# A feed-forward block in 7 products per pair: the second token pair's columns in reverse, a raw weight pair kept, and layer two's rows in step order

## Chip, cores and metric

One core of one Trainium2 chip. The metric is the device time of one launch in microseconds (us), lower is better; it is the median of several runs.

## What is computed

One decoder layer for one sequence of 2048 tokens and 1024 features, all float32:

```python
h = x + concat[rmsnorm(pool_mix(u)), rmsnorm(stick_breaking_attention(q, k, v))] @ w_out
h = h + relu(rmsnorm(h) @ w_up) ** 2 @ w_down      # d_ff = 4096: the FFN
y = rmsnorm(h)
```

The change lies in the second line, the FFN. "Layer one" is the product with `w_up`, "layer two" the product with `w_down`.

## The kernel before, in words

**Precision.** Every float32 operand of a product is split into a high and a low part (`split`, L143 to L147: ScalarE writes the high part, L146; VectorE the rest, L147), and each product takes three matmuls: high by high, high by low, low by high.

**Pairs of token tiles.** The tokens lie in four tiles of 512 (`T`). The FFN takes them as two pairs, `PAIRS = ((0, 1), (3, 2))`, and multiplies the 2 by 2 blocks of a pair by a 2 by 2 blocked weight with seven products (`P1` to `P7`) in place of eight, so sums and differences of operands (`S1` to `S4`, `A11`, `A12`, `A22`) are made, stored and loaded again. `q` is the pair, 0 or 1.

**Layer one, `up` (L861).** It runs over 32 columns, `cols`: for each pair `q`, the columns m = 0, 8, 1, 9, ..., 7, 15. A column has seven slots, one for each product, each of 12 matmuls of 128x128 by 128x512. For a column, `load` brings the raw weights `rb` (1 MB; one place for m below 8, one for the rest), two columns ahead; `make_weights` sums and splits them four slots ahead (`hw`). The left operands of a pair, `sa`, stay on chip for its 16 columns; `make_left` loads each as two tiles `sr` of 512 KB from `su` and splits them, five slots ahead of the first use, so at the turn from pair 0 to pair 1 fourteen loads and splits fall into the last column of the one and the first of the other. The pool `srp` of the `sr` tiles has three places of 4 KB.

`post` takes a product out of PSUM after its slot: copies `p1`, `u2`, `u3` on ScalarE (`copy`, L1007), the squared relu on ScalarE (L1001, L1002), sums on VectorE, each result in a 2 KB place of the pool `avp` (13 places), and a store to `sd`. For three of the operands (`A22`, `S1`, `A12`) the products of layer two are split a second time by the same scheme, with rows of pair 0 as the one half: in pair 1, `inner_row` loads their rows of pair 0 (`hr`, out of `sd[0]`), into the halves of one `srp` tile for the columns m and m + 8, and `inner_sums` makes from them and the new result what is stored to `sdi`.

While pair 0 runs, `weights_first` prepares part of layer two's weights (loads `t` and `b` of `w_down`, stores to `td` and `wi`) with tiles of `avp`.

**Layer two, `down` (L1090).** `steps` lists P1, P6, P7 with eight steps each over the inner blocks `kk`, in the order `TURN`, then three inner products of 28 steps, then P3. A step of P1, P6 or P7 has 48 matmuls. `make` loads its weights (`wr`) and its rows of both pairs (`ar`, out of `sd`, 512 KB each) and splits them. `make_ahead` makes up to three steps ahead of the one that is multiplied; `more_weights` (through the list `late`) prepares weights of later products. Step 0 is made early, at high priority; the rest of `make_ahead` is queued behind the last store of `S3` (`marks["up"]`, set in `post`).

**Places.** Layer two's pools lie over those of layer one: the first two places of `ar` (`rs`) over the raw weights, the other three (`rs2`) over `srp`, the second pool of split rows (`s82`) over the left operand of P3.

**What sets the order.** A scheduler that simulates the program orders the instructions of each engine; `tc.issue_after(ins)` only keeps what is in its block behind `ins` in the order of the same engine. Almost all DMAs of these stages are issued by SyncE (SP), in one order, and each engine works through its own list in order.

Of the kernel before, what the change touches and what calls it, by code (L numbers as in the profile page):

```python
# [8 lines left out]
F32 = mybir.dt.float32  # L9
# [6 lines left out]
P = 128  # L16
S = 2048
D = 1024
T = 512
# [18 lines left out]
LB = 4  # L38
# [8 lines left out]
def hymba_block(ctx: ExitStack, tc: tile.TileContext, xT, gains, w_in, pool_w, w_out, w_up, w_down, out):  # L47
    nc = tc.nc
# [87 lines left out]
    sd = [[[dram.tile([P, 2, T], F32, name=f"sd{q}_{i}_{c}") for c in range(8)] for i in range(7)] for q in range(2)]  # L136
# [6 lines left out]
    def split(dst, src):  # L143

        hi, lo = dst
        nc.scalar.activation(hi, src, AF.Copy)  # L146
        return nc.vector.tensor_tensor(lo, src, hi.bitcast(F32), ALU.subtract)  # L147
# [5 lines left out]
    marks, gates = {}, []  # L153
# [687 lines left out]
    A11, A12, A22, S1, S2, S3, S4 = range(7)  # L841
# [19 lines left out]
    def up(pools, more):  # L861

        saps, hlp, rba, rtp, srp = pools
        NM = NF // 2
        cols = [(q, m + x * (NM // 2)) for q in range(2) for m in range(NM // 2) for x in range(2)]
        halves = {}

        def inner_row(m, i):

            if m < NM // 2:  # L870
                halves[i, "rows"] = srp.tile([P, 2, T], F32, tag="sr", name="hr")
            nc.sync.dma_start(halves[i, "rows"][:, m // (NM // 2)], sd[0][i][m // 2][:, m % 2])

        def inner_sums(m, i, t):

            rows, at = halves[i, "rows"], m % (NM // 2)
            d, r = rows[:, 0], rows[:, 1]
            keep = lambda n, v: nc.sync.dma_start(sdi[i][n][at // 2][:, at % 2], v)
            if m < NM // 2:
                nc.vector.tensor_tensor(d, d, t, ALU.subtract)  # L880
                keep(2, d)
                halves[i] = t
                return
            a = halves.pop(i)
            nc.vector.tensor_tensor(a, a, t, ALU.add)
            keep(0, a)
            nc.vector.tensor_tensor(d, t, d, ALU.subtract)
            keep(1, d)
            nc.vector.tensor_tensor(r, r, d, ALU.subtract)
            keep(3, r)  # L890
# [5 lines left out]
        order = list(what)  # L896

        slots = [cols[0] + ("P1",)]
# [4 lines left out]
        raw, sums, ops, left_ops, ps, keep = {}, {}, {}, {}, {}, {}  # L903

        def load(q, m):
            raw[q, m] = (rbb if m >= NM // 2 else rba).tile([P, 4, G, P], F32, tag="rb", name="rb")
            nc.sync.dma_start(raw[q, m], w_up[m])

# [79 lines left out]
        def post(q, m, s):  # L988
            k = keep.setdefault((q, m), {})
            x, y, z = (ps.get((q, m, b)) for b in "XYZ")  # L990
            new = lambda name: avp.tile([P, T], F32, tag="av", name=name)

            def put(i, t, kept=None):
                if q == 0 or m >= NM // 2 or i not in (A12, A22, S1):
                    kept = nc.sync.dma_start(sd[q][i][m // 2][:, m % 2], t)
                if q and i in (A12, A22, S1):
                    inner_sums(m, i, t)
                return kept

            def act_of(i, src, t):  # L1000
                nc.scalar.activation(t, src, AF.Relu)  # L1001
                nc.scalar.activation(t, t, AF.Square)  # L1002
                k[i] = t

            def copy(name):
                k[name] = pup.tile([P, T], F32, tag=name, name=name)
                nc.scalar.activation(k[name], y, AF.Copy)  # L1007

            if s == "P1":
                copy("p1")  # L1010
            elif s == "P2":
                t = new("a11")
                nc.vector.tensor_tensor(t, x, k["p1"], ALU.add)
                act_of(A11, t, t)
                put(A11, t)
            elif s == "P6":
                if q:
                    for i in (A22, S1, A12):
                        inner_row(m, i)
                copy("u2")  # L1020
            elif s == "P7":
                copy("u3")
                t = new("a22")
                nc.vector.tensor_tensor(t, z, k["u3"], ALU.add)  # L1024
                act_of(A22, t, t)
                put(A22, t)
            elif s == "P4":
                t = new("a21")
                act_of("A21", y, t)
                k[S1] = new("s1")  # L1030
                nc.vector.tensor_tensor(k[S1], t, k[A22], ALU.add)
                put(S1, k[S1])
                k[S2] = new("s2")
                nc.vector.tensor_tensor(k[S2], k[S1], k[A11], ALU.subtract)
                put(S2, k[S2])
                nc.vector.tensor_tensor(t, k[A11], t, ALU.subtract)
                marks["up"] = put(S3, t)
            elif s == "P3":
                t = new("a12")
                nc.vector.tensor_tensor(t, z, k["u2"], ALU.add)  # L1040
                act_of(A12, t, t)
                put(A12, t)
                s4 = new("s4")
                nc.vector.tensor_tensor(s4, t, k[S2], ALU.subtract)
                put(S4, s4)
# [9 lines left out]
        yield  # L1055
        rbb, pup, avp, psu = more()
        load(*cols[1])
        first_weights = weights_first()
        lefts = [(g, q, s) for g, (q, m, s) in enumerate(slots) if m == 0 and not (q == 0 and s in order[:LB])]
        for g, (q, m, s) in enumerate(slots):  # L1060
            while lefts and lefts[0][0] <= g + LA:
                make_left(*lefts.pop(0)[1:])
# [4 lines left out]
            bank, first, last = what[s][2:]  # L1067
            if first:
                ps[q, m, bank] = psu.tile([P, T], F32, tag=bank, name="p" + bank)
            t, w = ps[q, m, bank], ops.pop(g)  # L1070
# [8 lines left out]
            elif g in (6, 10):  # L1079
                pr, i = psu.tile([P, T], F32, tag="R", name="pr"), g // 10  # L1080
                spread(pr, yrlast[:, i])
                nc.scalar.activation(rlast[:, i], pr, AF.Copy)
            if g + UA < len(slots):
                make_weights(g + UA)
                q2, m2, s2 = slots[g + UA]
                n = cols.index((q2, m2)) + 2
# [3 lines left out]
    def down(pools):  # L1090
        t8, s8, rs, rt, pupa, pup, rtx, rlp, tmp_, psb = pools

        SPLIT = {"P4": A22, "P5": S1, "P2": A12}
        TURN = (0, 4, 1, 5, 2, 6, 3, 7)
        order = (("P1", A11), ("P6", S2), ("P7", S3), ("P4", A22), ("P5", S1), ("P2", A12))
        steps = []
        for n, i in order:
            if n in SPLIT:
                steps += [(n, p, kk, None) for p in ("P1", "P5", "P6", "P3", "P7", "P2", "P4") for kk in range(4)]
            else:  # L1100
                steps += [(n, i, kk, (0, 1)) for kk in TURN]
        steps += [("P3", S4, kk, (q,)) for q in range(2) for kk in range(8)]
        made, turns = {}, {"ar": -2, "ad": 0}

# [27 lines left out]
        def blk(i, kk, where=None):  # L1132
            t = (where or rt).tile([P, 4, 256], F32, tag="wr", name="wr")
            nc.sync.dma_start(t, w_down[i, kk] if isinstance(i, int) else td[int(i[1]) - 1][kk])
            return t

        def minus(a, b):
            nc.vector.tensor_tensor(b, a, b, ALU.subtract)
            return b
# [30 lines left out]
        def make(g):  # L1170
            n, i, kk, qs_ = steps[g]
            if qs_ is None:
                made[g] = make_inner(n, i, kk)
                return
            b11, b12, b21, b22 = range(4)
            if n == "P1":
                w = blk(b11, kk)
            elif n == "P6":
                w = minus(blk(b22, kk), blk("t1", kk))
            elif n == "P7":  # L1180
                w = minus(blk(b22, kk), blk(b12, kk))
            else:
                w = blk(b22, kk)
            rows = {q: row([P, 2, T], F32, "ar") for q in qs_}
            for q in qs_:
                last[0] = nc.sync.dma_start(rows[q], sd[q][i][kk])
            t = t8.tile([P, 2, 4, 256], F32R, tag="wd", name="wd", align_bytes=256)
            split((t[:, 0], t[:, 1]), w)
            left_ = {}
            for q in qs_:  # L1190
                left_[q] = row([P, 2, 2, T], F32R, "ad", align_bytes=256)
                last[1] = split((left_[q][:, 0], left_[q][:, 1]), rows[q])
            while late and n != "P1":
                late.pop(0)()
            late.append(lambda: more_weights(n, kk, w))
            made[g] = t, left_
# [175 lines left out]
        free, held, ahead, late, last = 4, [], [0, 0, 0], [], [None, None]  # L1372
# [10 lines left out]
        def make_ahead(limit=len(steps)):  # L1383

            while ahead[0] < limit and (ahead[1] + lefts(ahead[0]) <= 6 and ahead[2] + stationary(ahead[0]) <= 3):
                make(ahead[0])
                ahead[1] += lefts(ahead[0])
                ahead[2] += stationary(ahead[0])
                ahead[0] += 1

        with tc.high_priority():
            make_ahead(1)
        with tc.issue_after(marks["up"].ins):
            make_ahead()
        for g, (n_, i, kk, qs_) in enumerate(steps):
            t, left_ = made.pop(g)
# [204 lines left out]
```

## Time and profile before

| what | value |
|---|---|
| median of 3 runs | 1921.9 us (1920.15 to 1922.53) |
| the profiled execution's own time | 1928.76 us |
| its span, first to last instruction | 1926.9 us |
| mean granted TensorE clock | 0.993 |
| PE (matmuls) busy | 1896.0 us, 98% |
| VectorE (DVE) / ScalarE (ACT) busy | 1423.0 us, 74% / 1006.2 us, 52% |
| moved by DMA | 511.78 MB, mean 266 GB/s |
| layer one in the trace | about 697 to 1318 us |
| turn from pair 0 to pair 1 | about 1003 us |
| layer two, to the end | from about 1318 us |

In the rows of the profile an engine's line gives start, duration, engine, line of the kernel, and out<-in by the names above; PE is the matmul, PEld its weight load, SPq the issuing of DMAs by SyncE. A bracket gives the idle time before an instruction and what ended it. Windows give the busy time of each engine in a stretch, the granted clock (PEclk, 1.00 is full) and the DMA engines' busy share and rate.

### The profile page before, as it was taken

How to read it: one execution, taken by the hardware profiler on the slowest of the kernel's cores; microseconds unless marked ns; L12 is line 12 of the kernel's file. 1: busy time of each engine (PE TensorE's matmuls, PEld its weight loads, DVE VectorE, ACT ScalarE, POOL GpSimd, SP SyncE). 2: the span in 40 equal slices, each digit the busy share in tenths (PEclk: the TensorE clock that was granted, in tenths of full speed). 3: DMA queues.
4: the chain of work that ended last, by engine and by line, in shares of the span. 5: the costliest groups of instructions: out<-in, count | busy, mean ns of one | idle time of the engine just before them, and what ended most of it. 6: DMA issues, size and time to landing. Idle time of an engine off the chain costs nothing.

```text
span 1926.9 us, 26520 instructions
## 1 busy us (share of the span) xinstructions
PE 1896.0 (98%) x8995; PEld 1581.0 (82%) x8995; DVE 1423.0 (74%) x2128; ACT 1006.2 (52%) x1598; POOL 177.3 (9%) x399
## 2 busy tenths in 40 slices
PE   9999999999999999999999999998999999999997
PEld 7888888887888888888878888886888888888886
DVE  6887799668866977777777877786655447888874
ACT  5565566555554465555566555454233345656543
POOL 0211123101211020000000000000010010020120
PEclk9999999999999999999999999999999999999999
DMA  6686686888797867776786777778998889899862
GB/s 213 206 268 195 201 284 219 259 303 266 268 337 283 299 219 265 279 242 224 275 306 237 265 251 259 247 264 307 357 362 293 279 260 311 287 298 342 295 208 90
DMA packets 206322, 511.78 MB, mean 266 GB/s; under 512 B 24288, under 2 KB 30432, under 8 KB 202080
## 3 DMA queue, kind: packets, MB, share of 16 engines
q1 hardware_dynamic: 201424, 501.33, 75.3%
q0 software_dynamic: 4608, 8.39, 2.4%
q8 instruction: 73, 1.20, 0.3%
q14 instruction: 73, 0.60, 0.1%
q10 hardware_dynamic: 144, 0.26, 0.0%
HBM read 337.92 MB, written 171.97 MB: 265 GB/s over the span
## 4 chain that ended last, share of the span: by engine, by line
PE 85%; DMA 7%; DVE 5%; issue 1%; ACT 1%; SPq 1%; POOL 0%; DVEq 0%; ACTq 0%
PE pb L1409 16%; PE pY L1074 15%; PE pb L1238 10%; PE pd L178 8%; PE pd L180 8%; PE pd L179 8%; PE pZ L1074 7%; PE pX L1074 4%; PE po L675 2%; DMA ar<-sd 1%; PE pta L664 1%; DMA t<-in_w_down_dram 1%; DMA ar<-sdi 1%; PE pm L205 1%; PE pr L231 1%
## 5 line engine op out<-in xcount | busy, mean ns | idle before, releaser
L1074 PE MATMUL pY<-sa,hw 128*128 128x512 f32 x1536 | 368.4, 391 | 4.0 <-ACT u L1007 4.0
L1409 PE MATMUL pb<-ad,wd 128*128 128x512 f32 x1488 | 342.6, 391 | 5.4 <-ACT ad L146 5.3
L1074 PEld LDWEIGHTS pY<-sa,hw 128*128 128x128 f32 x1536 | 289.9, 189 | 65.2 <-ACT u L1007 4.8
L1409 PEld LDWEIGHTS pb<-ad,wd 128*128 128x128 f32 x1488 | 279.5, 188 | 64.8 <-ACT ad L146 6.2
L178 PE MATMUL pd<-h,hl 128*128 128x512 f32 x752 | 299.6, 398 | 0.7 <-DVE qkr L424 0.7
L180 PE MATMUL pd<-h,hl 128*128 128x512 f32 x752 | 297.0, 395 | 0.0
L179 PE MATMUL pd<-h,hl 128*128 128x512 f32 x752 | 296.7, 395 | 0.0
L1238 PE MATMUL pb<-ad,wd 128*128 128x512 f32 x1008 | 228.9, 389 | 0.3 <-DVE ad L147 0.3
L1238 PEld LDWEIGHTS pb<-ad,wd 128*128 128x128 f32 x1008 | 189.1, 188 | 40.0 <-DVE ad L147 0.7
L147 DVE TENSOR_TENSOR ad<-ar,ad 128x1024 fp32r<-128x1024 f32 x148 | 179.5, 1221 | 51.8 <-ACT ad L146 51.8
L146 ACT ACTIVATE ad<-ar 128x1024 fp32r<-128x1024 f32 x148 | 155.1, 1052 | 102.3 <-issue 47.7
L1074 PE MATMUL pZ<-sa,hw 128*128 128x512 f32 x768 | 186.9, 390 | 0.6 <-DVE a L1024 0.6
L1074 PEld LDWEIGHTS pZ<-sa,hw 128*128 128x128 f32 x768 | 144.3, 188 | 31.0 <-DVE a L1024 1.1
L178 PEld LDWEIGHTS pd<-h,hl 128*128 128x128 f32 x752 | 142.2, 189 | 28.2 <-DVE qkr L424 1.0
L180 PEld LDWEIGHTS pd<-h,hl 128*128 128x128 f32 x752 | 141.9, 189 | 27.9
L179 PEld LDWEIGHTS pd<-h,hl 128*128 128x128 f32 x752 | 141.9, 189 | 27.1
L146 ACT ACTIVATE hl<-raw 128x512 fp32r<-128x512 f32 x168 | 104.2, 630 | 110.9 <-PE pd L180 68.8
L147 DVE TENSOR_TENSOR hl<-raw,hl 128x512 fp32r<-128x512 f32 x168 | 114.2, 686 | 55.0 <-ACT hl L146 51.8
L147 DVE TENSOR_TENSOR hw<-rt,hw 128x512 fp32r<-128x512 f32 x128 | 86.8, 685 | 56.4 <-ACT hw L146 56.4
L146 ACT ACTIVATE wd<-wr 128x1024 fp32r<-128x1024 f32 x40 | 42.4, 1060 | 125.9 <-PE pb L1409 99.3
L1001 ACT ACTIVATE a<-a 128x512 f32<-128x512 f32 x96 | 59.4, 630 | 88.4 <-DVE a L1040 40.1
L147 DVE TENSOR_TENSOR wd<-wr,wd 128x1024 fp32r<-128x1024 f32 x40 | 49.0, 1224 | 70.9 <-ACT wd L146 70.8
(219 smaller groups left out, 2696.6 us busy)
## 6 DMA issues: line engine op xcount, KB each, us to landing
ar<-sd SPq DMA_DIRECT2D x100, 512.0 KB, 5.5
rb<-in_w_up_dram SPq DMA_DIRECT2D x32, 1024.0 KB, 6.3
wr<-in_w_down_dram SPq DMA_DIRECT2D x64, 512.0 KB, 5.4
sd<-a SPq DMA_DIRECT2D x112, 256.0 KB, 4.2
raw<-in_w_in_dram SPq DMA_DIRECT2D x50, 512.0 KB, 4.3
ar<-sdi SPq DMA_DIRECT2D x48, 512.0 KB, 5.8
sd<-s SPq DMA_DIRECT2D x88, 256.0 KB, 4.4
sdi<-hr SPq DMA_DIRECT2D x72, 256.0 KB, 4.4
```

Source lines behind the costliest of these rows:

```text
L146: nc.scalar.activation(hi, src, AF.Copy)
L147: return nc.vector.tensor_tensor(lo, src, hi.bitcast(F32), ALU.subtract)
L178: nc.tensor.matmul(ps, hl[:, 0, c], hi, start=(k == 0), stop=False)
L179: nc.tensor.matmul(ps, hl[:, 0, c], lo, start=False, stop=False)
L180: mm = nc.tensor.matmul(ps, hl[:, 1, c], hi, start=False, stop=(k == n - 1))
L205: marks["pm"] = nc.tensor.matmul(pm[:, c:c + 1], ss[:, c * P:(c + 1) * P], inv[n], start=(i == 0), stop=(i == len(parts) - 1))
L231: mm = nc.tensor.matmul(pr[:, b * P:(b + 1) * P], yr[:, x, b:b + 1].to_broadcast([P, P]), identr, start=(b == 0 and x == 0), stop=(b == TB ...
L675: nc.tensor.matmul(po[:, p * 256 + to:p * 256 + to + hi - lo], vw[:, 2 * p + v], at[:, x, lo:hi], start=(p == 0 and n == 0 and x == 0), sk ...
L1001: nc.scalar.activation(t, src, AF.Relu)
L1074: nc.tensor.matmul(t, w[:, wx, c], a[:, ax, c % 2], start=first and c == 0 and x == 0, stop=last and c == G - 1 and x == 2, skip_group_che ...
L1238: nc.tensor.matmul(b, t[:, wx, 2 * (kk % 2) + c, i * P:(i + 1) * P], a[:, ax, c], start=p in ("P1", "P5", "P2") and kk == 0 and c == 0 and ...
L1409: nc.tensor.matmul(ps[q, n], block(t, wx, c, n), left_[q][:, ax, c], start=(n_ in ("P1", "P3") and kk == 0 and c == 0 and x == 0), stop=(n ...
```

## The change

Five things are done together.

- Pair 1 takes the columns in reverse: 7, 15, 6, 14, ..., 0, 8. Its first two columns are the last two of pair 0, so their raw weights are still on chip and `load` takes the tile that is there (no transfer).
- In these two first columns of pair 1 the rows `hr` go to 2 KB places of `avp` instead of halves of an `srp` tile. In the other columns nothing changes there.
- Layer two's P1, P6, P7 take their steps in the order 3, 7, 2, 6, 1, 5, 0, 4, which is the order in which pair 1 now finishes its rows. "First step" and "last step" are counted by place in the list, so `TURN` is looked up in `make`.
- Step 1 of layer two is made behind the last store of `A22` (`marks["A22"]`) and the rest behind that of `S3` (`marks["S3"]`); before, all but step 0 came behind that of `S3`.
- In P1 each row load is queued behind the row load of the operand before it.

```diff
-        cols = [(q, m + x * (NM // 2)) for q in range(2) for m in range(NM // 2) for x in range(2)]
+        cols = [(q, m + x * (NM // 2)) for q in range(2) for m in range(NM // 2)[::(1, -1)[q]] for x in range(2)]
...
-            if m < NM // 2:
-                halves[i, "rows"] = srp.tile([P, 2, T], F32, tag="sr", name="hr")
-            nc.sync.dma_start(halves[i, "rows"][:, m // (NM // 2)], sd[0][i][m // 2][:, m % 2])
+            if m == NM // 2 - 1:
+                halves[i, "rows"] = [avp.tile([P, T], F32, tag="av", name="hr")]
+            elif m == NM - 1:
+                halves[i, "rows"].append(avp.tile([P, T], F32, tag="av", name="hr"))
+            elif m < NM // 2:
+                t = srp.tile([P, 2, T], F32, tag="sr", name="hr")
+                halves[i, "rows"] = [t[:, 0], t[:, 1]]
+            nc.sync.dma_start(halves[i, "rows"][m // (NM // 2)], sd[0][i][m // 2][:, m % 2])
...
-            d, r = rows[:, 0], rows[:, 1]
+            d, r = rows[0], rows[-1]
...
         def load(q, m):
+            if q and m % (NM // 2) == NM // 2 - 1:
+                raw[q, m] = raw[0, m]
+                return
...
-                put(A22, t)
+                marks["A22"] = put(A22, t)
...
-                marks["up"] = put(S3, t)
+                marks["S3"] = put(S3, t)
...
-        lefts = [(g, q, s) for g, (q, m, s) in enumerate(slots) if m == 0 and not (q == 0 and s in order[:LB])]
+        lefts = [(g, q, s) for g, (q, m, s) in enumerate(slots) if (q, m) in ((0, 0), (1, NM // 2 - 1)) and not (q == 0 and s in order[:LB])]
...
-        TURN = (0, 4, 1, 5, 2, 6, 3, 7)
+        TURN = (3, 7, 2, 6, 1, 5, 0, 4)
...
-                steps += [(n, i, kk, (0, 1)) for kk in TURN]
+                steps += [(n, i, kk, (0, 1)) for kk in range(8)]
...
+            if n != "P3":
+                kk = TURN[kk]
...
-                last[0] = nc.sync.dma_start(rows[q], sd[q][i][kk])
+                with tc.issue_after(last[0].ins) if n == "P1" and last[0] else nullcontext():
+                    last[0] = nc.sync.dma_start(rows[q], sd[q][i][kk])
...
-        with tc.issue_after(marks["up"].ins):
+        with tc.issue_after(marks["A22"].ins):
+            make_ahead(2)
+        with tc.issue_after(marks["S3"].ins):
             make_ahead()
```

## The prediction, made before the change was run

> **What bounds the kernel now.** I read the page's first part, then who waited on PE, then PE's timeline in the two places that the change touches (the turn from pair 0 to pair 1, the passage from layer one to layer two), then what stood in front of the late operand there.
>
> ```profile
> PE 1896.0 (98%) x8995; PEld 1581.0 (82%) x8995; DVE 1423.0 (74%) x2128; ACT 1006.2 (52%) x1598; POOL 177.3 (9%) x399
> ```
> ```profile
> PE pb L1409 <- ACT ad L146: 5.3, 2, 4.0
> PE pY L1074 <- ACT u L1007: 4.0, 2, 3.3
> ```
>
> PE is the bound. The change adds and removes no matmul, so it can only win what PE loses by waiting and by the slow clock behind a wait, and can lose only where it makes new waits. The two largest waits lie where the change works: at the turn (L1074, 3.3 us at once) and at the passage (L1409, 5.3 us in two).
>
> ```profile
> 1002.94 2.88 PE L1074 MATMUL pX<-sa,hw 128*128 128x512 f32 x12
> 1009.14 5.49 PE L1074 MATMUL pY<-sa,hw 128*128 128x512 f32 x12 [3.32 <-ACT u L1007]
> ...
> 1022.99 5.60 PE L1074 MATMUL pY<-sa,hw 128*128 128x512 f32 x24
> ```
> ```profile
> 1315.01 2.88 PE L1074 MATMUL pZ<-sa,hw 128*128 128x512 f32 x12
> 1317.73 11.04 PE L1409 MATMUL pb<-ad,wd 128*128 128x512 f32 x48
> 1330.09 11.53 PE L1409 MATMUL pb<-ad,wd 128*128 128x512 f32 x48 [1.32 <-ACT ad L146]
> 1345.64 54.55 PE L1409 MATMUL pb<-ad,wd 128*128 128x512 f32 x232 [4.02 <-ACT ad L146]
> ```
> ```profile
> core 0: us, PE busy (x) PEld busy (x) DVE busy (x) ACT busy (x) POOL busy (x), PEclk, DMA share, GB/s
> 462.30:465.60 3.30, 3.30 (x10) 2.65 (x9) 2.67 (x4) 1.18 (x2) 0.00 (x0) 0.50 0.97 345
> 978.00:988.00 10.00, 10.00 (x46) 8.28 (x45) 6.78 (x12) 7.77 (x13) 0.00 (x0) 1.00 0.91 315
> 1001.00:1008.00 7.00, 4.82 (x22) 3.66 (x20) 4.60 (x7) 0.66 (x2) 0.00 (x0) 1.00 0.98 361
> 1315.60:1322.00 6.40, 6.40 (x30) 5.31 (x29) 5.35 (x9) 1.97 (x4) 0.00 (x0) 1.00 0.90 288
> 1328.00:1345.00 17.00, 12.24 (x52) 9.16 (x50) 7.35 (x6) 6.41 (x7) 0.00 (x0) 1.00 1.03 402
> 1345.60:1349.70 4.10, 4.06 (x11) 2.97 (x12) 4.08 (x4) 3.79 (x4) 0.00 (x0) 0.58 0.45 153
> ```
>
> Twelve matmuls take 2.72 us when nothing is late (1315.01 to 1317.73), so 24 take 5.44 and a layer-two step of 48 takes 10.88. From that, what PE loses:
>
> - The turn. The 12 of 1002.94 would hand over at 1005.66; the next come at 1009.14: 3.48 us. From 1009.14 to 1022.99 the timeline has 48 matmuls: 13.85 us in place of 10.88, 2.97 us lost to the half clock behind the wait. Together **6.45 us**.
> - The passage. Step 1 of layer two starts at 1330.09 in place of 1317.73 + 10.88 = 1328.61: 1.48 us. Step 2 starts 15.55 us behind step 1: 4.67 us more. Behind it the clock is 0.58 for 4.10 us: 0.42 x 4.10 = 1.72 us. Together **7.87 us**.
>
> So 14.32 us, 0.74% of the span, is all that can be won here.
>
> **The change part by part. The turn.** What came last there:
>
> ```profile
> 987.86 0.69 DVE L980 TENSOR_TENSOR t<-t,b 128x512 f32<-128x512 f32 x1 [2.07 <-DMA t<-in_w_down_dram]
> ```
> ```profile
> 991.46 4.42 DMA sr<-su
> ...
> 1000.35 7.17 DMA sr<-su
> ...
> 1007.54 1.06 ACT sa L146
> 1008.60 0.49 ACT u L1007
> ```
> ```profile
> 978.04 0.33 SPq L907 DMA_DIRECT2D rb<-in_w_up_dram  x1
> 996.21 0.33 SPq L907 DMA_DIRECT2D rb<-in_w_up_dram  x1
> ```
>
> PE waits for a PSUM bank that ACT has to copy out (`u`), and ACT, which works in order, stands in front of that copy at the split of a left operand whose load takes 7.17 us, against 4.42 for the one at 991.46. The two `rb` loads are the raw weights of pair 1's first two columns, exactly those that the change drops. The first stands ahead of the load of `t` for which DVE idles 2.07 us; at 315 GB/s its 1.05 MB is 3.3 us of DMA time, of which the chain can gain 2.07 (the idle time) and no more is counted. The second is ahead of the load at 1000.35; 1.05 MB at 361 GB/s is 2.9 us, and 7.17 less the 4.42 of the undisturbed one is 2.75; I take 2.75. The operand then lands at 1007.52 - 2.07 - 2.75 = 1002.7 in place of 1007.52, and with 1.06 and 0.49 of ACT the bank is free at 1004.3, ahead of 1005.66. If only the second counts, it is 1006.3 and 0.7 us stay. Gain 5.7 to 6.45 us; I take **6.2**. What is late next is the left operand of P7, of which the second half is loaded behind the same queue; it moves by the same amounts.
>
> **The `hr` rows.** Six of the 13 `avp` places are taken for parts of the first two columns. The row loads get a wait that they lacked: they read what pair 0 stored one and two columns before, not sixteen. On SP the left-operand loads, stores and the next `rb` stand behind them, and DVE's L880 waits for them; cover is a column of 19 us (7 slots of 2.72) against a landing of 4.2 us for the store and about as much for the load. So nothing for that, and for the fuller pool this row and this one:
>
> ```profile
> 804.24 2.11 PE L1074 MATMUL pZ<-sa,hw 128*128 128x512 f32 x8 [0.63 <-DVE a L1024]
> ```
> ```profile
> ar<-sd SPq DMA_DIRECT2D x100, 512.0 KB, 5.5
> ...
> sd<-a SPq DMA_DIRECT2D x112, 256.0 KB, 4.2
> ```
>
> At 804 `avp` also holds tiles that wait for loads (`sums_second`), and PE lost 0.6 us. The ends are 0 and a place that comes free only with a landed store, 4.2 us of ACT standing still. I take 0.6 as the nearest case: **-0.6 us**. It can't be a gain: before, nothing waited for `hr` in `srp`.
>
> **The passage, step 1.**
>
> ```profile
> 1315.63 0.38 SPq L995 DMA_DIRECT2D sd<-a  x1
> ...
> 1321.57 0.64 SPq L995 DMA_DIRECT2D sd<-a  x1
> 1322.26 0.56 SPq L1134 DMA_DIRECT2D wr<-in_w_down_dram  x1
> 1322.87 0.72 SPq L1186 DMA_DIRECT2D ar<-sd  x1
> ...
> 1324.11 0.43 SPq L1186 DMA_DIRECT2D ar<-sd  x1
> ```
>
> The store at 1315.63 is the last of `A22`, that at 1321.57 the last of `S3`: step 1's three loads can go 5.9 us sooner, at 1316. They cost SP 1.71 us of issuing (0.56, 0.72, 0.43), by which the stores that they pass (`S1`, `S2`, `S3`, `sdi`) go later; nobody reads those before P4 except step 2's places, below. DMA has room there (288 GB/s against 402 later). Landed 5.5 us behind the last issue, at 1323.2, split by three ACT pieces of 1.06, the first operands stand at about 1326.5, ahead of 1328.61. Gain **1.48 us**. ACT and DVE have idle time for the splits (1.97 of 6.40 us busy on ACT).
>
> **The passage, step 2.**
>
> ```profile
> 1334.50 10.02 DMA ar<-sd
> ```
>
> Its rows go at 1334.50 and need 10.02 us against a median of 5.5: the queue moves 402 GB/s. In the compiled order of the kernel before, a row load of step 3 and one of step 4 are issued ahead of them, and step 1's 1.57 MB are just before. Step 1's go early now, and the order kept in P1 puts the other two (1.05 MB) behind: 2.62 MB at 402 GB/s is 6.5 us. Landed at 1338.0, first split at 1339.1, needed at 1317.73 + 2 x 10.88 = 1339.5: no wait. If only step 1's share counts (3.9 us), it is 1341.7 and 2.2 us stay. I take 1 us left and no slow clock: gain 4.67 + 1.72 - 1.0 = **5.4 us** (ends 2.5 to 6.4: the lower with 2.2 us of wait and the slow clock kept). What is late next is step 3, with 10.9 us more to load 1.5 MB; the rows moved behind are its own and step 4's, and this covers them.
>
> A wait of 2 us can cost the clock too:
>
> ```profile
> 460.98 0.33 PE L231 MATMUL pr<-identr,yr 128*128 128x128 f32 x1 [2.05 <-DVE pc L629]
> ```
>
> 2.05 us of idle were followed by a clock of 0.50 (the row of 462.30). The Trainium skill ("TensorE: Matmul & The Clock Gate", Part 1) has the clock halved after an idle window of about 3.4 us, free-running. By that rule a remaining 2.2 us would bring no slow clock and the lower end would be 4.2 in place of 2.5; this row does not agree, so I keep 2.5.
>
> **Layer two's order and the rest.** `TURN` reversed reads pair 1's rows in the order in which they are now stored, as before, so it costs and gains nothing. One thing moves: the weights of P4's second product, first half, are now completed by the last step of P7 instead of the fourth, while before the last step completed those needed two inner steps (5.4 us) later. Weights are written when their step is made, three steps of 10.88 us ahead, and read a product (10.9 us) into P4; a load, a sum and a store of 4 to 6 us each fit into these 40 us.
>
> **Sum.** 6.2 - 0.6 + 1.48 + 5.4 = 12.5 us; I take 12, since a reordered program can open a small wait elsewhere. The profiled execution had 1928.76 us for a span of 1926.9; the median is 1921.9, 6.9 below, and I take the difference over unchanged: span 1915, median **1910**.
>
> **The rivals.**
>
> - *One of the two places closes only.* The passage stays bound by DMA (402 GB/s, share 1.03: moving loads forward fills a stretch that has 288 already), or the turn's next left operand is late in place of this one. Gain 5 to 8 us: 1914 to 1917, 1915.5 in the middle. For it: the queue really is full at the passage. Against: the bytes in front of step 2 do become fewer.
> - *Nothing changes.* The scheduler's new order leaves other loads in front of both; the waits keep their lengths. 1922.
> - *Slower: the `avp` places.* In the first two columns of pair 1 up to six of 13 places are long-lived, beside three kept results of the column before and seven of its own. Where ACT's relu finds no place it stands until a store lands (4.2 us), the bank behind it isn't copied out, and PE stops as it did at 1009.14: 6.45 us each with the slow clock. Two such stops (12.9) eat the gain; from the third on it is slower, 19.4 - 13.1 = 6 us: 1928. For it: 3 + 6 + 7 is above 13. Against: those seven aren't all held at once, and the kept rows of `A22` go before those of `A12`.
>
> **How the numbers follow.** A measurement of this kernel can tell about 0.2%, 3.8 us, from no change. Forecast (both places close, 1907 to 1913): 0.52. One closes: 0.23. Both are faster by over 0.2%: 0.75. Nothing: 0.08. Slower: 0.17. The low end is all 14.3 us and a bit of less DMA elsewhere, 1906.5; leaving out the slower case and little else, the range goes up to 1925.
>
> **What would show it.** Right: no PE gap over 1 us near 1006 and no clock under 1.00 between 1000 and 1020; `rb` issued 30 times, not 32; at the passage step 1 without a gap and step 2 with one under 2 us. The turn is wrong if the split of a left operand on ACT still waits over 3 us for `sr`; step 2 is wrong if its rows are still issued at 1334 or land 10 us later. The slower case would show as ACT L1001 waiting for DMA stores in the 40 us behind the turn, with PE gaps released by `u` or `p`.

## The result, and the profile after

The changed kernel takes 1913.34 us (median of 8 runs, 1911.12 to 1917.71). The kernel before takes 1921.38 (median of 8). The ratio is 0.9958, with a 95% interval of 0.9943 to 0.9972: about 8.1 us less. One run of layer two's half, further down, was slow (2300.66 us at a granted clock of 0.77) and is left out of that kernel's median and ratio. The profiled executions differ by 11.0 us, 1926.9 to 1915.9 us of span: 5.2 us of it in layer one (620.4 to 615.2 us from its first matmul to layer two's), 5.4 in layer two and 0.4 ahead of both.

Who waited on PE in the changed kernel (us in total, times, longest), and the first line of its page:

```profile
PE 1891.8 (99%) x8995; PEld 1577.8 (82%) x8995; DVE 1424.4 (74%) x2128; ACT 1006.7 (53%) x1598; POOL 177.7 (9%) x399
```
```profile
PE pb L1422 <- ACT ad L146: 1.2, 1, 1.2
...
PE pY L1082 <- ACT u L1015: 0.7, 1, 0.7
```

The two waits of 5.3 and 4.0 us are now 1.2 and 0.7. PE has the same 8995 matmuls and 4.2 us less of busy time, near the 2.97 and 1.72 us that the slow clock had taken. PE's timeline of the changed kernel at the turn and at the passage:

```profile
1003.78 2.88 PE L1082 MATMUL pX<-sa,hw 128*128 128x512 f32 x12
1006.50 2.88 PE L1082 MATMUL pY<-sa,hw 128*128 128x512 f32 x12
...
1309.40 2.88 PE L1082 MATMUL pZ<-sa,hw 128*128 128x512 f32 x12
1312.12 22.27 PE L1422 MATMUL pb<-ad,wd 128*128 128x512 f32 x96
1335.57 29.66 PE L1422 MATMUL pb<-ad,wd 128*128 128x512 f32 x128 [1.17 <-ACT ad L146]
```

1003.78 + 2.72 is 1006.50: nothing is lost at the turn. At the passage steps 0 and 1 run as one stretch of 96 matmuls and step 2 waits 1.17 us. ScalarE's timeline at the turn, the kernel before first, then the changed kernel, and two rows of the changed kernel's DMAs:

```profile
1007.54 1.06 ACT L146 ACTIVATE sa<-sr 128x1024 fp32r<-128x1024 f32 x1 [6.34 <-DMA sr<-su]
```
```profile
1003.10 1.07 ACT L146 ACTIVATE sa<-sr 128x1024 fp32r<-128x1024 f32 x1 [2.48 <-DMA sr<-su]
1004.06 0.58 ACT L1015 ACTIVATE u<-pY 128x512 f32<-128x512 f32 x1
```
```profile
rb<-in_w_up_dram SPq DMA_DIRECT2D x30, 1024.0 KB, 6.4
```
```profile
1327.71 6.72 DMA ar<-sd
```

ScalarE still stands at the split of a late left operand, now for 2.48 us in place of 6.34, but the copy `u` behind it is over at 1004.64, ahead of the 1006.50 at which PE needs the bank. The last row is step 2's first row load: it takes 6.72 us to land, against 10.02 before. Windows of the changed kernel, columns as in the prediction's. The first lies about as far ahead of the turn as the one there, some 25 us, and the second ends about as far ahead of ScalarE's copy. The other three are moved by 5.61 us, since layer two starts that much sooner:

```profile
978.00:988.00 10.00, 10.00 (x46) 8.29 (x45) 8.77 (x14) 7.65 (x13) 0.00 (x0) 1.00 0.77 266
996.00:1003.00 7.00, 7.00 (x33) 5.79 (x32) 7.00 (x10) 4.57 (x7) 0.00 (x0) 1.00 0.68 247
1309.99:1316.39 6.40, 6.40 (x30) 5.31 (x29) 5.61 (x10) 1.43 (x3) 0.00 (x0) 1.00 0.84 284
1316.39:1322.39 6.00, 6.00 (x28) 4.95 (x27) 4.86 (x6) 2.69 (x4) 0.00 (x0) 1.00 1.05 358
1322.39:1339.39 17.00, 15.71 (x67) 12.06 (x66) 7.40 (x7) 6.37 (x6) 0.00 (x0) 1.00 0.94 343
```

The DMA engines are less full at the turn (share 0.91 to 0.77 ahead of it, 0.98 to 0.68 in front of the copy). At the passage the last stretch falls from 402 to 343 GB/s and the one ahead of it rises from 335 to 358; the first stays as it was (288 and 284).

### The profile page after: what moved, and what is told of

Same layout as the page of the kernel before. It is cut to its first block, busy times and chain, and to the rows that moved or that the text cites. A ratio compares the mean times of both kernels' runs of the same rounds, so it can differ in the third digit from the quotient of the medians.

```text
span 1915.9 us, 26510 instructions
## 1 busy us (share of the span) xinstructions
PE 1891.8 (99%) x8995; PEld 1577.8 (82%) x8995; DVE 1424.4 (74%) x2128; ACT 1006.7 (53%) x1598; POOL 177.7 (9%) x399
## 4 chain that ended last, share of the span: by engine, by line
PE 89%; DMA 4%; DVE 4%; issue 1%; ACT 1%; POOL 0%; SPq 0%; DVEq 0%; ACTq 0%
PE pY L1082 16%; PE pb L1422 16%; PE pb L1249 12%; PE pZ L1082 8%; PE pd L178 8%; PE pd L180 8%; PE pd L179 8%; PE pX L1082 4%; PE po L675 2%; PE pta L664 1%; DMA xt<-in_xT_dram 1%; PE pr L231 1%; DMA t<-in_w_down_dram 1%; PE pm L205 1%; PE pz L617 1%; DMA wr<-in_w_down_dram 1%
## 5 line engine op out<-in xcount | busy, mean ns | idle before, releaser
L1082 PE MATMUL pX<-sa,hw 128*128 128x512 f32 x384 | 93.1, 389 | 0.0
```

The lines of the kernel that those rows point to most:

```text
L1082: nc.tensor.matmul(t, w[:, wx, c], a[:, ax, c % 2], start=first and c == 0 and x == 0, stop=last and c == G - 1 and x == 2, skip_group_che ...
```

## The experiments

My theory was that two things gain separately: dropping two raw-weight loads frees the turn, and early loads of step 1 with ordered row loads free the passage. The rivals: one of them gives nothing, or the gain belongs to another part of the change. The idle times below are those in PE's brackets; some expectations count a wait from start to start of single matmuls, which is about 0.4 us more (3.70 for 3.32). Gains are (1 - ratio) x 1921.4.

| kernel | ratio to before, 95% | gain, us |
|---|---|---|
| the whole change | 0.9958 (0.9943 to 0.9972) | 8.1 |
| layer one's half only | 0.9992 (0.9979 to 1.0004) | 1.5 |
| the same, raw weights loaded again | 0.9999 (0.9989 to 1.0010) | 0.2 |
| layer two's half only (early step 1 and order) | 0.9971 (0.9960 to 0.9982) | 5.6 |
| early step 1 only | 1.0000 (0.9989 to 1.0011) | 0.0 |
| order of P1's row loads only | 0.9962 (0.9948 to 0.9976) | 7.3 |
| the change without the early step 1 | 0.9960 (0.9946 to 0.9973) | 7.7 |
| the change, step 1's splits later | 0.9953 (0.9939 to 0.9966) | 9.0 |
| the same, one split of step 0 later too | 0.9949 (0.9934 to 0.9964) | 9.8 |

**Layer one's half only.** Columns in reverse, raw weights reused, `hr` in `avp`, layer two's rows in the reversed order; of the change this is taken out:

```diff
-                with tc.issue_after(last[0].ins) if n == "P1" and last[0] else nullcontext():
-                    last[0] = nc.sync.dma_start(rows[q], sd[q][i][kk])
+                last[0] = nc.sync.dma_start(rows[q], sd[q][i][kk])
...
-        with tc.issue_after(marks["A22"].ins):
-            make_ahead(2)
```

> Layer one's half of the change alone (columns of pair 1 in reverse, their first two raw weights kept, first hr rows in avp, TURN reversed to match); step 1 of layer two stays behind the last S3 store and no order is kept among P1's row loads. My theory: the two places add up. The turn's wait (6.45 us in the trace of before) is gone, the passage's 7.87 us stay: in a profiled execution some 6 us less than before. Unprofiled the whole change won 8.1 us (ratio 0.9958), so I expect 3.5 to 6 us here, ratio 0.9969 to 0.9982. Rival 1: the passage alone carries it, ratio 0.999 to 1.001. Rival 2: the two hang together (a passage reached earlier with the same DMA work gives the gain back), under 2 us here.

Measured: 1919.68 us. PE's timeline at the turn, and who waited on PE at the passage:

```profile
999.69 1.98 PE L1082 MATMUL pX<-sa,hw 128*128 128x512 f32 x8
1001.51 2.88 PE L1082 MATMUL pY<-sa,hw 128*128 128x512 f32 x12
```
```profile
PE pb L1419 <- ACT ad L146: 4.9, 2, 3.1
```
```profile
1319.99 12.83 PE L1419 MATMUL pb<-ad,wd 128*128 128x512 f32 x48 [1.81 <-ACT ad L146]
```

The last row is step 1 of layer two. No wait at the turn, the passage as late as before (4.9 us against 5.3). So the turn is free by this half, as predicted. But the time falls by 1.5 us only, not by the expected 3.5 to 6, and the interval takes in no gain at all.

**Layer two's half only.** The kernel before with `make_ahead(2)` behind the last store of `A22` and P1's row loads in order:

```diff
-                last[0] = nc.sync.dma_start(rows[q], sd[q][i][kk])
+                with tc.issue_after(last[0].ins) if n == "P1" and last[0] else nullcontext():
+                    last[0] = nc.sync.dma_start(rows[q], sd[q][i][kk])
...
-        with tc.issue_after(marks["up"].ins):
+        with tc.issue_after(marks["A22"].ins):
+            make_ahead(2)
+        with tc.issue_after(marks["S3"].ins):
```

> Layer two's half alone: step 1 behind the last A22 store, row loads of P1 kept in order; columns, raw weight loads and hr places as before. My theory: the turn keeps its 3.4 us wait and the slow clock, the passage falls from 7.87 us lost to about 2: some 5.9 us less profiled, 3 to 6 us less unprofiled, ratio 0.9969 to 0.9984. Rival 1: it carries all 8 us, ratio 0.9958. Rival 2: the turn carries all and this shows no change, 0.999 to 1.001.

Measured: 1915.05 us. This half carries most of the gain, with waits of 0.4 and 1.3 us left at the passage. Its layer one has the same instructions in the same order on every engine as the kernel before, and yet PE's late matmul at the turn reads:

```profile
1006.47 3.01 PE L1075 MATMUL pY<-sa,hw 128*128 128x512 f32 x12 [0.83 <-ACT u L1008]
```

0.83 us where the profile before had 3.32, and 3.01 us for the 12 matmuls where it had 5.49, so no slow clock either. That opened the question of whether the turn's 6.45 us belong to the kernel or to that one execution. Both kernels were profiled again.

> The kernel before, unchanged, for a second profiled execution. The profiles of before and after differ by 11.0 us of span, the medians of the timed runs by 8.0. Theory A: a profiled execution of before always pays more for waits that hang on DMA, so this span is again 1925 to 1928 with 3.0 to 3.6 us of PE wait at the turn and 4 us at step 2. Theory B: the first profile of before was a long one by chance; this span is 1920 to 1923 and the two waits are shorter by 2 to 4 us together.

> The changed kernel, unchanged, for a second profiled execution. Theory A of before_again (profiled waits are longer in both): span 1915 to 1917, step 2's wait 1.0 to 1.4 us, no wait at the turn. Theory B (spread between executions): the span may lie anywhere from 1909 to 1917 and the difference is in waits that hang on DMA.

Measured: 1924.54 us and 1916.32 us. The changed kernel again has no wait at the turn, and its wait at step 2 is 0.3 us in place of 1.17. The kernel before has the span of theory B (1922.7 us) with the waits of theory A: what differs from its first profile lies ahead of layer one, which starts at 691.8 in place of 697.3 us. PE's timeline of the kernel before in this second profile:

```profile
998.75 2.88 PE L1074 MATMUL pX<-sa,hw 128*128 128x512 f32 x12
1004.36 5.49 PE L1074 MATMUL pY<-sa,hw 128*128 128x512 f32 x12 [2.72 <-ACT u L1007]
...
1018.25 1.98 PE L1074 MATMUL pY<-sa,hw 128*128 128x512 f32 x8
```

And, with what was expected, in a third:

> The kernel before once more. Theory (the wait at the turn is not fixed by the program but differs from one execution to the next): a wait of anything from 0.5 to 3.5 us at 1005, and step 2 of layer two waits over 3.5 us again, which is fixed by the order of the row loads. Rival (the turn's wait belongs to the program): 3.1 to 3.7 us start to start as in the two profiles of this kernel so far, with the half clock behind it.

```profile
999.89 2.88 PE L1074 MATMUL pX<-sa,hw 128*128 128x512 f32 x12
1004.68 3.04 PE L1074 MATMUL pY<-sa,hw 128*128 128x512 f32 x12 [1.92 <-ACT u L1007]
```

That execution took 1922.21 us. So the wait at the turn is 3.32, 2.72 and 1.92 us in three executions of one and the same program, with the slow clock behind the first two and without it behind the third, as the theory had it. The wait at step 2 is the same in all three (4.0, 4.1 and 4.2 us longest).

**The two parts of layer two's half, each alone.** Of the diff above, the first is the last block only, the second is the first block only.

> The kernel before with one part: step 1 of layer two is made behind the last A22 store instead of the last S3 store. Row loads of P1 keep the scheduler's order, columns as before. Layer two's half as a whole gave ratio 0.9971 (5.6 us). My theory for the passage: step 1's wait (1.5 to 2 us) goes, step 2 keeps the loads of steps 3 and 4 in front of its rows and so most of its wait: 2 to 3.5 us won, ratio 0.9982 to 0.9990. Rival: taking 1.6 MB out of the full stretch is all that counts, ratio 0.9965 to 0.9975.

> The kernel before with the other part: the row loads of P1 are kept in step order, step 1 stays behind the last S3 store. My theory: step 2's rows move ahead of 1.05 MB (2.6 us at 402 GB/s), so its wait of 4 us falls to 1.5 to 2 and with it the slow clock behind it (1.7 us) goes in most executions; step 1's wait stays: 2.5 to 4.5 us won, ratio 0.9977 to 0.9987. Rival: the rows' places set the time, not the order, and step 2 waits as long: ratio 0.9995 to 1.0005.

Measured: 1922.06 us and 1916.26 us. PE's timeline with the early step 1 alone:

```profile
1005.50 3.02 PE L1075 MATMUL pY<-sa,hw 128*128 128x512 f32 x12 [1.61 <-ACT u L1008]
...
1311.28 21.92 PE L1414 MATMUL pb<-ad,wd 128*128 128x512 f32 x96
1339.17 21.00 PE L1414 MATMUL pb<-ad,wd 128*128 128x512 f32 x79 [5.97 <-ACT ad L146]
```

With the order alone:

```profile
1006.80 4.35 PE L1075 MATMUL pY<-sa,hw 128*128 128x512 f32 x12 [3.47 <-ACT u L1008]
...
1019.45 0.84 PE L1075 MATMUL pY<-sa,hw 128*128 128x512 f32 x3
...
1314.18 11.04 PE L1413 MATMUL pb<-ad,wd 128*128 128x512 f32 x48
1327.83 32.34 PE L1413 MATMUL pb<-ad,wd 128*128 128x512 f32 x133 [2.60 <-ACT ad L146]
```

Early loads alone close step 1's wait and lengthen step 2's from 4.02 to 5.97: what is saved in front of one step is paid in front of the next, and the time is the same. (Theory and rival both expected a gain.) The order alone takes step 2's wait away, although step 1 is still late, and by the medians brings nearly the whole gain, more than the 2.5 to 4.5 us expected; the rival's unchanged time did not come. Why, SP's row loads and weight loads show, the kernel before first, then the one with the order alone:

```profile
1331.33 0.32 SPq L1186 DMA_DIRECT2D ar<-sd  x1
1331.93 1.00 SPq L1134 DMA_DIRECT2D wr<-in_w_down_dram  x2
1333.88 2.89 SPq L1186 DMA_DIRECT2D ar<-sd  x4
```
```profile
1328.55 5.34 SPq L1190 DMA_DIRECT2D ar<-sd  x4
1333.94 0.90 SPq L1135 DMA_DIRECT2D wr<-in_w_down_dram  x2
```

and ScalarE's splits of these rows, in the same order of kernels:

```profile
1344.54 4.85 ACT L146 ACTIVATE ad<-ar 128x1024 fp32r<-128x1024 f32 x5 [1.43 <-DMA ar<-sd]
```
```profile
1335.60 1.06 ACT L146 ACTIVATE ad<-ar 128x1024 fp32r<-128x1024 f32 x1 [0.17 <-DMA ar<-sd]
1336.87 1.06 ACT L146 ACTIVATE ad<-ar 128x1024 fp32r<-128x1024 f32 x1 [0.20 <-DMA ar<-sd]
1338.14 1.06 ACT L146 ACTIVATE ad<-ar 128x1024 fp32r<-128x1024 f32 x1 [0.21 <-DMA ar<-sd]
```

In the kernel before, one row load of a later step and two loads of weights that are needed later, and in the compiled order the first of the next four row loads too, go ahead of step 2's rows. When the row that ScalarE stands at lands, the others are there already, so five splits follow back to back. With the order the rows land one by one, 1.27 us apart, in the order in which they are split. Counted from the start of layer two (1317.73 and 1314.18), step 2's first split comes at 21.4 us in place of 26.8: its row load is issued 2.4 us sooner (1334.50 and 1328.55) and takes 7.0 us to land in place of 10.0. ScalarE's own order is not what held it, since the bracket in the kernel before has it waiting for that load.

**The raw weights loaded again.** Layer one's half, with this taken out:

```diff
-            if q and m % (NM // 2) == NM // 2 - 1:
-                raw[q, m] = raw[0, m]
-                return
```

> As up_only (reverse columns, hr in avp, layer two otherwise as before), but the raw weights of pair 1's first two columns are loaded again. Tells whether the dropped 2 MB closed the turn or the reordering around it. Theory: the loads; the turn waits 1 to 3.5 us in its trace, as in the executions of before and down_only (which have one and the same order of instructions up to layer two and waited 3.5, 2.9 and 1.0 us), and the time is 1920 to 1921, 0 to 1.5 us above up_only. Rival: the order; no wait at the turn, the same time as up_only (1919.7).

Measured: 1921.21 us, and on PE at the turn:

```profile
1001.28 3.06 PE L1079 MATMUL pY<-sa,hw 128*128 128x512 f32 x12 [1.00 <-ACT u L1012]
```

With the loads the wait is there again, without them it is not. The times (0.9999 and 0.9992) are too close to tell apart, and the turn's wait differs between executions. But all 14 profiles of this case agree: counted from start to start as in the prediction, PE loses 0.0 to 0.3 us in front of the late matmul in the seven that keep the raw weights, and 1.0 to 3.6 us in the seven that load them again. Of these seven this kernel is the only one with the reversed columns, so the split between the loads and the reordering rests on its one profile.

**The change without the early step 1**, and **with `hr` in `srp` as before**:

```diff
-        with tc.issue_after(marks["A22"].ins):
-            make_ahead(2)
```

> The changed kernel with all of make_ahead but step 0 queued behind the last store of S3 again; layer one's half and the order of P1's row loads are kept. Theory (the early step 1 gives nothing of its own, the order carries the passage): about 0.9960 of the time before, at most 1 us above the changed kernel, though the trace shows a wait of 1.5 to 3 us at step 1. Rival (the early step 1 is needed once the order is kept): step 1 waits 2.8 us and the slow clock behind it takes another 1.7, so 3 to 4.5 us above the changed kernel, ratio 0.9975 to 0.998.

```diff
-            if m == NM // 2 - 1:
-                halves[i, "rows"] = [avp.tile([P, T], F32, tag="av", name="hr")]
-            elif m == NM - 1:
-                halves[i, "rows"].append(avp.tile([P, T], F32, tag="av", name="hr"))
-            elif m < NM // 2:
+            if m < NM // 2:
```

> The changed kernel with the hr rows in srp halves as before, no avp places for them. Theory (the 2 KB places neither crowd avp nor save anything that PE sees): PE's waits between 1000 and 1060 are as in the changed kernel, none over 1 us, and the time is within 2 us of it. Rival (the srp places were what held the left operands' loads at the turn): an sr load is issued late behind an hr tile's release and PE waits 1 to 3 us near 1005 or 1025.

Measured: 1915.13 us for the first (ratio 0.9960) and 1913.38 us for the second, one run. PE's timeline of the first at step 1, and of the second behind the turn:

```profile
1313.61 11.04 PE L1420 MATMUL pb<-ad,wd 128*128 128x512 f32 x48
1326.23 23.99 PE L1420 MATMUL pb<-ad,wd 128*128 128x512 f32 x103 [1.59 <-ACT ad L146]
```
```profile
1020.43 0.73 PE L1078 MATMUL pY<-sa,hw 128*128 128x512 f32 x2 [1.01 <-ACT p L1011]
```

Without the early step 1 there is one wait of 1.59 us at step 1 and none at step 2; the time is that of the change within the noise, as the theory had it. With `hr` in `srp` nothing waits at the turn, and one wait of 1.01 us stands 15 us behind it. The rival had such a wait, but at another place, and in one profile it can't be told from chance (the change without the early step 1, with `hr` in `avp`, has one of 0.65 us at 1024). In this one run the places of `hr` show no effect on the time.

**Step 1's splits later.** In the changed kernel ScalarE takes step 1's weight split ahead of the last column's relu:

```profile
1315.80 1.06 ACT L146 ACTIVATE wd<-wr 128x1024 fp32r<-128x1024 f32 x1 [4.94 <-DMA wr<-in_w_down_dram]
1316.77 0.62 ACT L1009 ACTIVATE a<-a 128x512 f32<-128x512 f32 x1
```

```diff
-        with tc.issue_after(marks["A22"].ins):
+        with tc.issue_after(marks["A22"].ins), tc.issue_after(marks["relu"].ins), tc.issue_after(marks["sum"].ins):
```

(the marks stand at that relu and at the last sum on VectorE).

> The changed kernel with one addition: the splits of step 1 are queued behind the last column's relu on ACT and behind its last sum (s4) on DVE. The order on SP and PE is the changed kernel's. In its trace the split of step 1's weights stood on ACT and DVE in front of the last column's relu and sums and waited 4.9 us for its load, so the places for step 2's rows came free late and step 2 waited 1.2 us. Theory: step 2's wait goes (0 to 0.4 us), 1 to 2 us won against the changed kernel, 1911.5 to 1912.5, ratio to before 0.9950 or a little under. Rival: DMA bounds step 2 and nothing changes (1913.3, ratio 0.9958), or step 1 becomes late by the splits and it is 1 us slower.

```diff
-                last[1] = split((left_[q][:, 0], left_[q][:, 1]), rows[q])
+                with tc.issue_after(marks["u3"].ins) if g == 0 and q else nullcontext():
+                    last[1] = split((left_[q][:, 0], left_[q][:, 1]), rows[q])
```

> The changed kernel with step 1's splits behind the last column's relu and sum (as in split_behind), and the second pair's row split of step 0 behind the last copy u3 on ScalarE. Theory (the wait of 0.85 us at 1306 is ScalarE's u standing behind step 0's splits): that wait goes, and step 0 doesn't become late, since it is multiplied 10 us later; 0 to 2 us below the changed kernel, ratio 0.9945 to 0.996. Rival: the copy is late for another reason, or step 0's second pair becomes late in place of it: the same time as the changed kernel or up to 2 us more, with a wait at 1318.

Measured: 1913.89 us (0.9953) and 1912.24 us (0.9949). PE's timeline with the first, then ScalarE's and PE's with the second:

```profile
1310.05 36.16 PE L1422 MATMUL pb<-ad,wd 128*128 128x512 f32 x158
```
```profile
1302.21 0.60 ACT L1015 ACTIVATE u<-pY 128x512 f32<-128x512 f32 x1 [0.26 <-PE pY L1082]
```
```profile
1302.86 3.02 PE L1082 MATMUL pY<-sa,hw 128*128 128x512 f32 x12 [0.69 <-ACT u L1015]
```

The first removes the passage's last wait from the trace: layer two runs through. The second aimed at the wait of 0.69 us that follows and missed: ScalarE is idle for 0.26 us until PE ends `pY`, copies it, and PE has nothing else to do until that bank is free. Step 0's splits had no part in it; this wait comes from two slots on one bank behind each other. The intervals of these two and of the change overlap nearly whole, so a gain over the change is likely by the trace and not shown by the times.

**Layer two in all the profiles.** From its first matmul to the end of the span (1926.9 - 1317.73 in the kernel before) layer two takes 609.2 to 610.8 us in the six profiles without the order of the row loads: the kernel before three times, layer one's half, the same with the weights loaded again, and the early step 1 alone (610.7). With the order it takes 601.2 to 606.5 us in all eight: 603.5 and 606.5 without the early step 1, 602.0 to 604.4 with it, 601.2 and 601.9 with the later splits. The two groups don't meet, whatever else was changed. The early step 1 gives nothing without the order and little beside it.

## Why the prediction was right, and where it was not

**The direction and the two places.** PE's losses at the turn and at the passage were what could be won, and both closed: no gap near 1006, no slow clock there, 30 loads of `rb`, steps 0 and 1 without a gap, step 2 with one under 2 us. These are the signs that the prediction named. Its span of 1915 met 1915.9, in part by luck: both first profiles were late by about the same amount ahead of layer one (it starts at 697.3 and 697.0 us, in the other twelve profiles at 691.8 to 696.6), and the dear turn that was priced was the one of that very profile. The median came at 1913.3 for 1910, just outside the 1907 to 1913 given for both places closing, though the traces show that both closed.

**The turn: the mechanism right, the term too large.** 6.2 us were taken from one execution. Six executions of that same instruction order (three of the kernel before, and the three kernels that change layer two alone) lose 6.45, 5.9, 5.4, 2.1, 1.8 and 1.0 us there, slow clock included: 3.8 us in the mean. (Worked out as in the prediction. 5.9: 998.75 + 2.72 to 1004.36, and 13.89 us to 1018.25 for 48 matmuls; 5.4: 3.63 us of gap and 12.65 us from 1006.80 to 1019.45; the others have no slow clock, as the 3.0 us of their 12 matmuls show.) In the timed runs layer one's half is worth 1.5 us alone, 0.4 us beside the order (0.9962 to 0.9960), 2.5 us beside all of layer two's half (0.9971 to 0.9958), each with some 3 us of uncertainty. The profile that I worked from was the dearest case.

**`hr` in `avp`: -0.6 not found.** In the changed kernel's first profile no wait over 1 us shows on PE behind the turn in layer one, and the slower rival, three such stops, did not come.

**Step 1, 1.48 us: this step failed.** Counted as a gain of its own, it is none while step 2 waits: early loads alone gave 1.0000 and 5.97 us at step 2. Beside the order they are worth 0.4 us (0.9960 to 0.9958), which the runs can't tell from nothing.

**Step 2, 5.4 us: about right in size, wrong in its shares.** I gave step 1's early bytes 3.9 us and the order 2.6 us. The order alone does it. What I overlooked is in SP's rows above: besides two row loads, two loads of weights that are needed later stood ahead of step 2's rows. Four loads are 2.1 MB, at 402 GB/s 5.2 us, and the first split came 5.4 us sooner. By the times the order is worth 7.3 us (4.6 to 10.0); its one profile explains 3.1 of them: of the 7.87 it keeps a gap of 2.77 at step 1 (1314.18 + 10.88 to 1327.83) and 2.0 of slow clock behind it (32.34 us for 133 matmuls, 30.3 undisturbed). That execution took 1922.58 us, 6.3 above the median of its kernel. The change without the early step 1 has the same order of row loads and the same late step 1; in its profile the wait at step 1 is 1.59 us, no slow clock follows, and layer two is 3.0 us shorter (603.5 to 606.5). The faster runs of the order alone have no trace.

**From profile to median: failed.** I subtracted a constant 6.9 us. Three profiled executions of the kernel before lie 7.4, 3.7 and -0.1 us above the median of their runs (1928.76, 1924.54, 1922.21 against 1921.38, 1920.82, 1922.31), the changed kernel's first 4.4. The turn accounts for part of this only. Layer one starts at 697.3, 691.8 and 693.7 us in these three and takes 620.4, 621.2 and 617.2 us, while layer two takes 609.2 to 609.8. So the first differs from the second ahead of layer one, where the change does nothing, and from the third there and in layer one. To carry the distance over was to take the gain of one dear profile for that of the median: 12 us were counted where runs hold 8.1. What makes the stretch ahead of layer one longer or shorter was not looked into.

## What to carry to other kernels

Where several loads of one kind wait in one queue, look first at whether they go in the order in which they are needed: here that single edit was worth 7.3 of 8.1 us by the medians (4.6 to 10.0), and making one step early was worth nothing as long as the next stayed late. A wait that hangs on a transfer can differ between executions (at the turn) or stay the same (at step 2), and one profile doesn't tell which: take two or three of the same program before giving it a price, and don't carry a profile's distance to the median over to the next kernel. Give a wait's slow clock a price of its own, since it may or may not follow.

## What the runs showed of the hardware

**A wait costs the clock by where it lies.** In the traces the slow stretches are 3.41 us long, or twice that. Windows of that length, the kernel before (third profile) at the turn, then layer one's half alone at step 1 of layer two and, in the same profile, ahead of layer one; PE's busy time is the figure behind the first comma, the granted clock the third from the end:

```profile
1000.88:1004.29 3.41, 1.89 (x9) 1.23 (x7) 1.49 (x4) 1.20 (x2) 0.00 (x0) 1.00 1.03 416
1004.29:1007.70 3.41, 3.02 (x13) 2.50 (x14) 3.41 (x5) 3.41 (x7) 0.00 (x0) 1.00 0.66 210
```
```profile
1317.20:1320.60 3.40, 1.58 (x8) 1.00 (x7) 1.86 (x2) 2.11 (x2) 0.00 (x0) 1.00 1.02 402
1320.62:1324.02 3.40, 3.40 (x10) 2.42 (x9) 1.80 (x2) 1.82 (x2) 0.00 (x0) 0.50 1.05 414
```
```profile
453.63:457.04 3.41, 1.55 (x9) 0.95 (x7) 3.35 (x7) 1.93 (x4) 2.83 (x9) 1.00 0.73 203
457.04:460.45 3.41, 2.75 (x18) 2.52 (x19) 2.13 (x5) 1.09 (x2) 1.33 (x4) 1.00 1.02 346
```

The wait of 1.92 us was split by the border of two such windows, PE was busy for 1.89 us of the first, and the clock stayed full. The wait of 1.81 us (late matmul at 1319.99) lay in one window, PE was busy for 1.58 us of it, and the next window had half the clock. So between 1.58 and 1.89 us of busy time lies the dividing line in these two pairs of rows, near half of the window. It is no rule for the whole kernel: in the last pair PE was busy for 1.55 us and the clock stayed full. The Trainium skill ("TensorE: Matmul & The Clock Gate", Part 1) has a free-running window of 3413 ns, with which the length of the slow stretches agrees. It puts the slow clock behind an idle window, and its advice is no idle gap over about 3.4 us; the rows differ, a gap of 1.81 us was enough.

**The same instruction order, another wait.** With the same instructions in the same order up to the turn, its wait went from 0.83 to 3.47 us between executions, while that at step 2 stayed within 0.2 us in the kernel before. It isn't the chip alone: on one chip it was 1.61 and 3.47 us (the two parts of layer two's half), on another 0.83 and 2.72 (that half and the second profile of before). At the turn of the third profile the DMA engines moved 416 GB/s at a share of 1.03, in the changed kernel 247 at 0.68. That a full queue lets small differences through to PE fits these rows and is not shown: at step 2 the queue was as full (402 GB/s, 1.03) and the wait stayed the same. What differs from one execution to the next wasn't found.
